# Matmul, scale and add: one tile's results sent in eleven small transfers, and one move done whole

## The chip, the cores and the metric

The kernel runs on one core of one Trainium2 chip. The metric is the device time of one execution in microseconds; the kernel before has a median of 209.18 us over three runs (209.13 to 209.81).

## The reference

`x` is 16 × 512 × 1024, `weight` 1024 × 768, `add_value` 16 × 512 × 768, all float32; `scale` is 0.1.

```python
def reference(x, weight, scale, add_value):
    return (scale * np.matmul(x, weight) + add_value).astype(np.float32)
```

Flattened, it is one product of 8192 × 1024 by 1024 × 768, scaled, with a matrix of the same shape as the result added.

## The kernel before, in words

The 8192 rows are 64 tiles of 128 rows. They lie in three blocks of 24, 24 and 16 tiles. Within a block a partition holds consecutive rows of the matrix, so that a transfer of n neighbouring tiles is 128 contiguous runs of n × 4096 bytes (`x`) or n × 3072 bytes (`add_value` and the results).

**The stream.** All large transfers are written out in `STREAM` (lines 22 to 25): `x0+4` loads tiles 0 to 3 of x, `a` stands for `add_value`, `w` for the weight, `o` for results. SyncE issues them in that order on its one queue (`sync_engine`, line 120). Ahead of an issue it waits, where needed, for the transfer eight places earlier (`lanes`), for the moves that free a slot of x, for the results that free a slot of `ao`, or, ahead of an `o`, for the results to be made (`made`). `x` has 16 tile slots (`xs`). `add_value` and the results share 32 tile slots (`ao`): the result overwrites what was added. The last entry, `o60+4`, is issued on line 243, behind the end of the critical section in which all engines run their own instruction lists, and so behind the last instruction of each engine.

**The moves.** ScalarE and GpSimd (`mover`, line 140) cast x to bf16 and rearrange it into one of two buffers `va`, four tiles (one move q, 0 to 15) at a time; each of the two engines does half of the blocks. A move is eight instructions of 32 partitions and four tiles. Moves listed in `HALVED` (line 17: 0, 1 and 10) are done in two halves of two tiles, sixteen instructions, so that the first two tiles are ready sooner.

**Turn and finish.** VectorE (line 160) transposes two tiles of `va` into `xt` (`turn`), and later makes two tiles of results (`finish`): product × scale + `add_value`, written in place into `ao`, which counts up `made`.

**The product.** TensorE (line 219) runs a loop over the tiles: for each tile 8 steps over k, with two matmuls a step (512 and 256 columns), and releases two tiles at a time through `done`.

A transfer's completion adds 16 to its semaphore. The functions that the change touches:

Of the kernel before, what the change touches and what calls it, by code (L numbers as in the profile page):

```python
# [7 lines left out]
P = 128  # L8
# [5 lines left out]
MM_BUFS = 4  # L14
XT_TILES = 4
LANES = 8
HALVED = (0, 1, 10)
TURN_FIRST = (0, 24)
VA_BUFS = 2
MOVE = 4  # L20

STREAM = """
    x0+4 w0+8 x4+8 a0+8 a8+8 x12+4 x16+8 a16+8 x24+8 a24+8 x32+8 o0+8 o8+8 a32+8 x40+8
    a40+8 x48+8 x56+4 o16+8 o24+8 a48+4 x60+4 a52+4 a56+8 o32+16 o48+4 o52+8 o60+4
"""


# [7 lines left out]
def kernel(  # L35
# [22 lines left out]
    def blocks(flat):  # L58
        return [(s, g, flat[P * s:P * (s + g), :].rearrange("(p t) n -> p t n", t=g))
                for s, g in BLOCKS]  # L60

    x_v, add_v, out_v = blocks(x_f), blocks(add_f), blocks(out_f)
    w_v = weight.rearrange("(p r) n -> p r n", p=P)

    def rows(view, s, n):
        for first, g, block in view:
            if first <= s and s + n <= first + g:
                return block[:, s - first:s - first + n, :]
        raise ValueError((s, n))
# [5 lines left out]
    ao = const.tile([P, A_SLOTS, N], fp32, name="ao")  # L75
    w_bf = const.tile([P, KJ, N], bf16, name="w_bf")
    RUN = K // 4
    va = [const.tile([P, MOVE, 4, RUN], bf16, name=f"va{i}") for i in range(VA_BUFS)]
    xt = const.tile([P, XT_TILES, KC, P], fp32, name="xt")
# [5 lines left out]
    by_act, by_pool, pool_go, turned, casts, done, made = (  # L85
        tc.alloc_semaphore(name)
        for name in ("by_act", "by_pool", "pool_go", "turned", "casts", "done", "made"))
    TURNED = MOVE * VA_BUFS
    MADE = TURNED + MM_BUFS

    def carriers(op, s, n):
        return [mark for (o, a, k), mark in zip(stream, landed)
                if o == op and a < s + n and s < a + k]

    def slots(op, s, n):
        ring = X_SLOTS if op == "x" else A_SLOTS
        k = s % ring
        assert k + n <= ring
        return slice(k, k + n)

    def engine(eng):
        known = {}

        def need(sem, value):
            if known.get(id(sem), 0) < value:
                eng.wait_ge(sem, value)  # L106
                known[id(sem)] = value

        return need

    def transfer(eng, op, s, n):
        if op == "w":
            return eng.dma_start(ao[:, W_SLOT + s:W_SLOT + s + n, :], w_v[:, s:s + n, :])  # L113
        if op == "x":
            return eng.dma_start(xs[:, slots(op, s, n), :], rows(x_v, s, n))  # L115
        if op == "a":
            return eng.dma_start(ao[:, slots(op, s, n), :], rows(add_v, s, n))  # L117
        return eng.dma_start(rows(out_v, s, n), ao[:, slots(op, s, n), :])

    def sync_engine(eng):  # L120
        need = engine(eng)
        for (op, s, n), (sem, mark) in zip(stream, landed):
# [13 lines left out]
            if op == "o":  # L136
                need(made, MADE + last)
            transfer(eng, op, s, n).then_inc(sem, 16)

    def mover(eng, copy, parity, count, go=None):  # L140
        need = engine(eng)
        if go is None:
            eng.preload_act_table(mybir.ActivationFunctionType.Copy)  # L143
        for q in range(MOVES):
            for mark in carriers("x", MOVE * q, MOVE):
                need(*mark)
            if q >= VA_BUFS:
                need(turned, TURNED + MOVE * (q - VA_BUFS + 1))
            if go is not None:
                eng.sem_inc(go, 1)  # L150
            k = MOVE * q % X_SLOTS
            src = xs[:, k:k + MOVE, :].rearrange("p i (b k) -> p i b k", b=4)
            step = MOVE // 2 if q in HALVED else MOVE
            for t in range(0, MOVE, step):
                for a in (parity, parity + 2):
                    for b in range(4):
                        copy(va[q % VA_BUFS][32 * b:32 * b + 32, t:t + step, a, :],  # L157
                             src[32 * a:32 * a + 32, t:t + step, b, :]).then_inc(count, step // 2)

    def vector_engine(eng):  # L160
        need = engine(eng)

        def cast_w(s, n):
            for mark in carriers("w", s, n):
                need(*mark)
            for h in range(s, s + n, 4):
                eng.tensor_copy(w_bf[:, h:h + 4, :], ao[:, W_SLOT + h:W_SLOT + h + 4, :]).then_inc(casts, 4)  # L167

        def turn(pair):
            move, half = divmod(pair, 2)  # L170
            moved = 16 * move + (8 * (half + 1) if move in HALVED else 16)
            need(by_act, moved)
            need(by_pool, moved)
            if pair > 1:
                need(done, 4 * (pair - 1))
            pairs = va[move % VA_BUFS][:, 2 * half:2 * half + 2, :, :].bitcast(fp32)
            eng.transpose(  # L177
                xt[:, 2 * half:2 * half + 2, :, :].rearrange("p i c (a m) -> p i c a m", a=4),
                pairs.rearrange("p i a (k c) -> p i c a k", c=KC),
            ).then_inc(turned, 2)  # L180

        def finish(pair):
            for mark in carriers("a", 2 * pair, 2):
                need(*mark)
            need(done, 4 * (pair + 1))
            a = ao[:, slots("a", 2 * pair, 2), :]
            q = 2 * (pair % 2)
            eng.scalar_tensor_tensor(  # L188
                a, mm[:, q:q + 2, 0:N], float(scale), a,
                op0=mybir.AluOpType.mult, op1=mybir.AluOpType.add).then_inc(made, 2)  # L190

        turn(0)
        for op, s, n in stream:
            if op == "w":
                cast_w(s, n)
        turn(1)
        for pair in range(T // 2):
            ahead = pair + 2 < T // 2
            if ahead and pair in TURN_FIRST:
                need(done, 4 * (pair + 1))  # L200
                turn(pair + 2)
            finish(pair)
            if ahead and pair not in TURN_FIRST:
                turn(pair + 2)
# [14 lines left out]
    def tensor_engine(eng):  # L219
        eng.sem_inc(turned, TURNED)  # L220
        eng.sem_inc(made, MADE)
        eng.wait_ge(casts, KJ)
# [14 lines left out]
    with tc.tile_critical(no_gpsimd_drain=True):  # L237
        sync_engine(nc.sync)
        mover(nc.scalar, nc.scalar.copy, 0, by_act)
        mover(nc.gpsimd, nc.gpsimd.tensor_copy, 1, by_pool, pool_go)  # L240
        vector_engine(nc.vector)
        tensor_engine(nc.tensor)
# [36 lines left out]
```

## Time and profile before

| | |
|---|---|
| median of three runs | 209.18 us |
| profiled execution, its own time | 209.87 us |
| its span | 208.1 us |
| mean granted TensorE clock | 0.981 |
| busy: TensorE, VectorE, ScalarE, GpSimd | 81%, 59%, 67%, 67% |
| data moved | 87.06 MB, 418 GB/s over the span |

Times in the profile count from the start of the span. A row of the timeline gives the start, the duration, the engine, the line and the operation, and in brackets how long the engine was idle before and what released it; "SPq" is the queue work of SyncE, whose instructions here are the issues of transfers. A row of stretches gives the stretch, its length, then busy time and number of instructions for TensorE, its weight loads, VectorE, ScalarE and GpSimd, then the granted clock, the mean busy share of the 16 transfer engines (DMA engines), and GB/s. In the DMA view the digits are the busy share of these engines in 40 equal slices, "packets" are the single pieces that they process, and packets under 512 B are completion signals of 4 bytes. q1 is the queue that SyncE issues on, and q14 carries the fetching of instructions. A group row gives the busy time and the mean duration in ns after the bar, and then idle time with its releasers.

### The profile page before, as it was taken

The page shows a single profiled execution, that of the slowest core. Times are in us where ns is not written, and L with a number is a line of the kernel's source. Part 1 is how long each engine was busy: PE and PEld are TensorE (multiplying, and loading weights), DVE is VectorE, ACT ScalarE, POOL GpSimd, SP SyncE. Part 2 cuts the span into 40 slices and gives each one's busy share as a digit, 9 for nine tenths or more (in the row PEclk, how much of TensorE's full clock was granted, in tenths as well). Part 3 has the DMA queues.
Part 4 walks back from the last instruction along what each step waited for, and adds up shares of the span by engine and source line. Part 5 has one row for each costly group of instructions (what it writes and reads, how often), then busy time and mean ns, then how long its engine had stood idle before and what let it go on. Part 6 is the DMA issues. An engine that isn't in the chain of part 4 may idle for free.

```text
span 208.1 us, 2174 instructions
## 1 busy us (share of the span) xinstructions
PE 167.7 (81%) x1008; PEld 50.4 (24%) x512; DVE 122.9 (59%) x66; ACT 139.3 (67%) x153; POOL 139.9 (67%) x156
## 2 busy tenths in 40 slices
PE   0001994969999999999999999994999999999500
PEld 0000231313333333333333333321333333333100
DVE  0037309646777777777777777738677759776300
ACT  2495199989799896969694069999998969000000
POOL 0399399999799997969694059999999979000000
PEclk9999999999999999999999999999999999999975
DMA  6999999999999999999999999999999999998993
GB/s 249 452 408 447 409 453 444 409 457 403 436 461 409 425 463 416 367 411 439 439 427 438 419 441 450 403 428 447 435 409 432 427 439 449 449 453 364 454 411 161
DMA packets 4035, 87.06 MB, mean 418 GB/s; under 512 B 448, under 2 KB 448, under 8 KB 448
## 3 DMA queue, kind: packets, MB, share of 16 engines
q1 hardware_dynamic: 4032, 87.03, 97.9%
q14 instruction: 3, 0.02, 0.0%
HBM read 61.87 MB, written 25.17 MB: 418 GB/s over the span
## 4 chain that ended last, share of the span: by engine, by line
DMA 43%; PE 25%; POOL 21%; issue 3%; DVE 2%; SPq 1%; POOLq 0%; DVEq 0%
DMA xs<-in_x_dram 31%; POOL va L157 21%; PE mm L232 16%; DMA out_dram<-ao 12%; PE mm L207 9%; DVE xt L177 1%; DVE ao L188 1%; SPq L115 0%; SPq L113 0%; SPq L117 0%; POOLq L150 0%; SPq L106 0%; DVEq L106 0%; SPq L274 0%; SPq L237 0%
## 5 line engine op out<-in xcount | busy, mean ns | idle before, releaser
L232 PE MATMUL mm<-w_bf,xt 128*128 128x512 bf16 x496 | 163.8, 382 | 26.9 <-DVE w_bf L167 19.8
L157 POOL CAST va<-xs 32x1024 bf16<-32x1024 f32 (+1 forms) x152 | 139.7, 919 | 36.8 <-DMA xs<-in_x_dram 22.4
L157 ACT CAST va<-xs 32x1024 bf16<-32x1024 f32 (+1 forms) x152 | 138.0, 908 | 36.6 <-DMA xs<-in_x_dram 23.4
L207 PE MATMUL mm<-w_bf,xt 128*128 128x256 bf16 x512 | 140.2, 274 | 0.8
L232 PEld LDWEIGHTS mm<-w_bf,xt 128*128 128x128 bf16 x512 | 50.4, 98 | 144.6 <-issue 138.7
L177 DVE STREAM_TRANSPOSE xt<-va 128x1024 f32<-128x1024 f32 x32 | 65.2, 2038 | 32.0 <-POOL va L157 30.6
L188 DVE SCALAR_TENSOR_TENSOR ao<-mm,ao 128x1536 f32<-128x1536 f32 x32 | 56.0, 1754 | 42.5 <-PE mm L207 39.4
L167 DVE CAST w_bf<-ao 128x3072 bf16<-128x3072 f32 x2 | 3.8, 1948 | 0.0
L143 ACT ACT_TABLE_LOAD x1 | 1.3, 1283 | 0.9 <-SPq L237 0.9
L260 POOL MEMSET const-float32-0.0<- 128x1 f32 x1 | 0.1, 98 | 0.2 <-issue 0.2
L260 POOL MEMSET const-bfloat16-1.0<- 128x1 bf16 x1 | 0.1, 101 | 0.0
L260 POOL MEMSET const-float32-1.0<- 128x1 f32 x1 | 0.1, 98 | 0.0
L260 POOL MEMSET const-uint8-127<- 128x1 uint8 x1 | 0.1, 98 | 0.0
## 6 DMA issues: line engine op xcount, KB each, us to landing
xs<-in_x_dram SPq DMA_DIRECT2D x6, 4096.0 KB, 20.8
ao<-in_add_value_dram SPq DMA_DIRECT2D x7, 3072.0 KB, 25.2
out_dram<-ao SPq DMA_DIRECT2D x5, 3072.0 KB, 24.8
xs<-in_x_dram SPq DMA_DIRECT2D x4, 2048.0 KB, 13.3
out_dram<-ao SPq DMA_DIRECT2D x1, 6144.0 KB, 33.9
ao<-in_weight_dram SPq DMA_DIRECT2D x1, 3072.0 KB, 14.1
ao<-in_add_value_dram SPq DMA_DIRECT2D x2, 1536.0 KB, 14.6
out_dram<-ao SPq DMA_DIRECT2D x2, 1536.0 KB, 19.8
```

What stands on the lines that cost most here:

```text
L143: eng.preload_act_table(mybir.ActivationFunctionType.Copy)
L157: copy(va[q % VA_BUFS][32 * b:32 * b + 32, t:t + step, a, :], src[32 * a:32 * a + 32, t:t + step, b, :]).then_inc(count, step // 2)
L167: eng.tensor_copy(w_bf[:, h:h + 4, :], ao[:, W_SLOT + h:W_SLOT + h + 4, :]).then_inc(casts, 4)
L177: eng.transpose(xt[:, 2 * half:2 * half + 2, :, :].rearrange("p i c (a m) -> p i c a m", a=4), pairs.rearrange("p i a (k c) -> p i c a k", ...
L188: eng.scalar_tensor_tensor(a, mm[:, q:q + 2, 0:N], float(scale), a, op0=mybir.AluOpType.mult, op1=mybir.AluOpType.add).then_inc(made, 2)
L207: return eng.add_instruction(mybir.InstMatmult(name=nc.get_next_instruction_name(), engine=eng.engine, ins=[eng.lower_ap(weights), eng.low ...
L232: eng.matmul(mm[:, q, 0:CUT], piece, w_bf[:, j, 0:CUT], **flags)
L260: nc = _bacc.Bacc("TRN2", target_bir_lowering=False, num_devices=1)
```

## The change

Tile 47 is taken out of the transfer of results `o32+16`, which becomes `o32+15`. Its 128 rows (one per partition, 3,072 bytes each) are sent by eleven transfers of their own, issued by ScalarE (nine: partitions 5 to 39, four at a time, the last with three) and by GpSimd (two: partitions 0 to 4, and 40 to 127), each behind its last move. Both engines wait for `made` to cover tile 47 first, and for their transfers to land afterwards. They are dealt with the aim that one of the 16 transfer engines gets a single row of tile 47. In the same edit move 10 (tiles 40 to 43) is no longer done in halves.

```diff
-HALVED = (0, 1, 10)
+HALVED = (0, 1)
 TURN_FIRST = (0, 24)
+SPREAD = 47
+BY_ACT = [(a, min(a + 4, 40)) for a in range(5, 40, 4)]
+BY_POOL = [(0, 5), (40, P)]
...
-    a40+8 x48+8 x56+4 o16+8 o24+8 a48+4 x60+4 a52+4 a56+8 o32+16 o48+4 o52+8 o60+4
+    a40+8 x48+8 x56+4 o16+8 o24+8 a48+4 x60+4 a52+4 a56+8 o32+15 o48+4 o52+8 o60+4
...
+    spread_act, spread_few, spread_many = (
+        tc.alloc_semaphore(name) for name in ("spread_act", "spread_few", "spread_many"))
+
+    def spread(eng, a, b):
+        return eng.dma_start(rows(out_v, SPREAD, 1)[a:b], ao[a:b, slots("o", SPREAD, 1), :])
...
+        need(made, MADE + SPREAD + 1)
+        if go is None:
+            for a, b in BY_ACT:
+                spread(eng, a, b).then_inc(spread_act, 16)
+            need(spread_act, 16 * len(BY_ACT))
+        else:
+            for (a, b), sem in zip(BY_POOL, (spread_few, spread_many)):
+                spread(eng, a, b).then_inc(sem, 16)
+            need(spread_few, 16)
+            need(spread_many, 16)
```

The added lines of the last part stand at the end of `mover`, behind its loop; `go` is None for ScalarE.

## The prediction

> **What bounds the kernel now.** I read the page's slices and DMA queues first, then the timeline of each engine from 160 us on, and last the DMA view of short windows at the end of the span.
>
> ```profile
> span 208.1 us, 2174 instructions
> ...
> DMA  6999999999999999999999999999999999998993
> GB/s 249 452 408 447 409 453 444 409 457 403 436 461 409 425 463 416 367 411 439 439 427 438 419 441 450 403 428 447 435 409 432 427 439 449 449 453 364 454 411 161
> DMA packets 4035, 87.06 MB, mean 418 GB/s; under 512 B 448, under 2 KB 448, under 8 KB 448
> ...
> q1 hardware_dynamic: 4032, 87.03, 97.9%
> q14 instruction: 3, 0.02, 0.0%
> ```
>
> The sixteen transfer engines are busy from the first slice to the last: 97.9% of 16 engines' span is packets of the one queue. So the kernel ends when its bytes are through, as long as the last results reach the queue before it runs dry. These rows say that they do:
>
> ```profile
> 154.02 1.76 DVE L188 SCALAR_TENSOR_TENSOR ao<-mm,ao 128x1536 f32<-128x1536 f32 x1 [1.49 <-PE mm L207]
> 168.25 8.52 ACT L157 CAST va<-xs 32x1024 bf16<-32x1024 f32 x8 [1.88 <-DVE xt L177]
> 168.29 8.69 POOL L157 CAST va<-xs 32x1024 bf16<-32x1024 f32 x8 [0.90 <-DVE xt L177]
> 195.62 1.76 DVE L188 SCALAR_TENSOR_TENSOR ao<-mm,ao 128x1536 f32<-128x1536 f32 x1 [3.44 <-PE mm L207]
> 197.66 0.33 SPq L118 DMA_DIRECT2D out_dram<-ao  x1
> ```
>
> VectorE makes the last two tiles by 195.62 + 1.76 = 197.38; the last transfer (tiles 60 to 63) is issued at 197.66. Now the end of the span, in three windows of the DMA view (from 205.3, from 206.1 and from 206.3 us, each to the end; forty slices each, the GB/s of a slice counting the packets that start in it), and stretches ahead of them:
>
> ```profile
> 203.00:204.00 1.00, 0.00 (x0) 0.00 (x0) 0.00 (x0) 0.00 (x0) 0.00 (x0) 0.50 0.98 418
> 204.40:204.80 0.40, 0.00 (x0) 0.00 (x0) 0.00 (x0) 0.00 (x0) 0.00 (x0) 0.50 0.58 246
> 204.80:205.20 0.40, 0.00 (x0) 0.00 (x0) 0.00 (x0) 0.00 (x0) 0.00 (x0) 0.50 0.22 92
> ```
> ```profile
> DMA  4008004004000000400000000000000000000000
> GB/s 176 0 0 351 0 0 176 0 0 176 0 0 0 0 0 0 176 0 0 0 0 0 0 0 0 0 0 0 0 0 0 0 0 0 0 0 0 0 0 0
> DMA packets 9, 0.07 MB, mean 26 GB/s; under 512 B 3, under 2 KB 3, under 8 KB 3
> ...
> DMA packets 3, 0.01 MB, mean 6 GB/s; under 512 B 2, under 2 KB 2, under 8 KB 2
> ...
> DMA packets 2, 0.01 MB, mean 7 GB/s; under 512 B 1, under 2 KB 1, under 8 KB 1
> ```
>
> Until 204.4 all engines move data; after 204.8 about a fifth do. From 205.3 on nine packets start: six of 12,288 bytes (a partition's row of the last transfer, four tiles of 3,072) and three that only signal completion. Three engines are thus late. A slice of the first window is 0.07 us, so the six begin near 205.3, 205.5 (two), 205.7, 205.9 and 206.4. The spacing 205.5, 205.9, 206.4 is one engine's, 0.46 us a packet; it ends at 206.4 + 0.46 = about 206.9 us. The packet at 205.7 ends the second engine at about 206.2 (one signal starts between 206.1 and 206.3), the other one at 205.5 the third at about 206.0. The other thirteen are done before 205.3, most near 204.8. The kernel waits 0.7 us for one engine alone, and some 2 us for three. Its span ends 208.1 − 206.9 = 1.2 us behind the last packet.
>
> The profiled execution took 209.87 us, 1.8 more than its span; the median of the runs is 209.18, 0.69 below. I take the difference that the sum gives from the median.
>
> **Part 1, tile 47 in small transfers.** A row of one tile is 3,072 bytes: at 12,288 bytes in 0.46 us, 0.115 us of an engine. Removed: o32+16 becomes o32+15, each of whose 128 rows is 0.115 us shorter. With 128/16 = 8 rows on each engine that is 8 × 0.115 = −0.92 us everywhere. Added: the same 128 rows, one of them to one engine. That engine's balance is −0.92 + 0.115 = −0.8 us; the other fifteen carry 127 rows, 8.5 each, hence 0 for an engine with eight and +0.23 for one with ten.
>
> By the Trainium skill, page "DMA: Bandwidth & Descriptors", section "Why a DMA increments its semaphore by 16 and not by 1", a transfer runs on the largest number of engines up to 16 that divides its outer size: 4, 3, 5 and 11 here, the lowest-numbered ones for ScalarE's transfers and consecutive ones for GpSimd's. By that rule, if GpSimd's begin at engine 0, engines 0 to 2 get ten rows, engine 3 nine, engine 4 one and engines 5 to 15 eight; no run here shows it yet.
>
> Which engine of the sixteen is the late one no view names. If it is the one with a single row, it ends at 206.9 − 0.8 = 206.1, and the second then sets the end: 206.2 plus what eight separate rows cost above one piece of the same bytes. That price has no row. From below it is 0: a packet of 12 KB moves at the pace of the larger ones (418 GB/s at a share of 0.98 in the stretch 203 to 204; the page's mean is 418 GB/s at 97.9%). From above, the nearest row of a packet that comes in from another queue is an instruction fetch of 8 KB (first fence below: window 58.8 to 59.2; then windows 53.88 to 54.2, 61.3 to 62.2 and 61.65 to 62.2):
>
> ```profile
> q14 instruction: 2, 0.02, 11.8%
> ...
> DMA packets 2, 0.02 MB, mean 77 GB/s; under 512 B 1, under 2 KB 1, under 8 KB 1
> ...
> DMA packets 15, 0.43 MB, mean 473 GB/s; under 512 B 2, under 2 KB 2, under 8 KB 2
> ...
> DMA packets 13, 0.39 MB, mean 715 GB/s; under 512 B 1, under 2 KB 1, under 8 KB 1
> ```
>
> Two fetches take 11.8% of 16 × 0.4 us, 0.76 us, or 0.38 each; 8 KB at the pace above is 0.31, so 0.07 us too many per packet at the least. At 53.88 one completion signal is left; after the fetches two come past 61.3 and one of these past 61.65, which is where the late engine's lag begins. The lag is about half a microsecond more than before, at most 0.2 us per fetch beyond its bytes. So a row's surcharge lies between 0 and 0.2 us. I take 0.01, near the lower end, because rows are packets of the same direction and kind as their neighbours while a fetch is not: 8 × 0.01 = +0.1 us. The second engine then ends at 206.3, and the gain is 206.9 − 206.3 = 0.6 us.
>
> **What the new instructions wait for.** Both movers come to the new lines behind their last move, at 168.25 + 8.52 = 176.8 (ScalarE) and 177.0 (GpSimd); tile 47 is in the results made at 154.02 (pair 23), 20 us before. ScalarE then issues nine transfers; with SP's 0.33 us each (row above) that is 3.0 us, to about 180, on an engine with no other work left. GpSimd issues two. Their price on GpSimd is not in the trace; between 0.3 and a few microseconds it ends by 185. Nothing stands behind these instructions but the end of the critical section, at which SP sends the last transfer. The two waits therefore cost nothing if the rows land before 197.4. The SP queue holds o32+15 (rows of 46 KB, 15 × 0.115 = 1.7 us each, eight per engine), then o48+4 and o52+8. If an engine takes one packet from each queue in turn, nine rows pass while nine or ten large packets do: until about 177 + 9 × 1.7 = 192. The cover is 5 us, and 2 more, since the last transfer's eight packets (3.7 us) begin at 204.5 − 3.7 = 200.8 on the fastest engines, though issued at 197.66. If the cover were gone, each microsecond past about 199 would lengthen the run by one.
>
> **Part 2, tiles 40 to 43 moved whole.**
>
> ```profile
> L157 POOL CAST va<-xs 32x1024 bf16<-32x1024 f32 x104 | 107.6, 1034 | 12.9 <-DVE xt L177 5.7 <-DMA xs<-in_x_dram 1.2
> L157 POOL CAST va<-xs 32x512 bf16<-32x512 f32 x48 | 32.2, 670 | 24.0 <-DMA xs<-in_x_dram 21.3
> ...
> 127.17 2.05 DVE L177 STREAM_TRANSPOSE xt<-va 128x1024 f32<-128x1024 f32 x1 [0.25 <-POOL va L157]
> 141.26 2.01 DVE L177 STREAM_TRANSPOSE xt<-va 128x1024 f32<-128x1024 f32 x1 [3.91 <-POOL va L157]
> ...
> 140.00:143.30 3.30, 0.66 (x5) 0.10 (x1) 2.04 (x2) 3.23 (x4) 3.12 (x4) 1.00 1.00 425
> ...
> 170.57 1.76 DVE L188 SCALAR_TENSOR_TENSOR ao<-mm,ao 128x1536 f32<-128x1536 f32 x1 [2.43 <-DMA ao<-in_add_value_dram]
> ```
>
> The first half of tile 40's move ends at 127.1, so the move began 8 × 0.67 = 5.4 us earlier, near 121.75, and lasts 10.7 in halves; whole it lasts 8 × 1.03 and gaps, 8.7 us: to 130.5. Tiles 40 and 41 are transposed 3.3 us later (130.5 in place of 127.17), so TensorE stalls some 2.7 us near 130. Tiles 44 to 47 are moved 2 us earlier, and the stall of 2.6 us between 140 and 143.3 closes. Sum: within 0.3 us of nothing at 143. And near 170 VectorE waits 2.43 us for a transfer, which resets TensorE's lead whatever it was. The loads that wait for this move (x56) come 2 us earlier into a queue that is full. Cost 0; without the cover of the full queue it would be those 0.3 us.
>
> **Sum.** −0.6 + 0 + 0: 209.18 − 0.6 = 208.6 us.
>
> **The rivals.**
>
> *Rows cost more than their bytes (slower).* Place: the second late engine, or one with ten rows. With a surcharge s an engine of eight rows ends at 206.2 + 8 s; it decides from s = 0.7/8 = 0.09 us, above which the run gets longer than before. At s = 0.2 it ends at 207.8, +0.9: 210.1 us. For it speaks the fetch's 0.07 to 0.2; against it, the 12 KB packets at full pace.
>
> *The rows wait for whole transfers (slower).* If an engine empties what SP queued of one transfer before it takes another queue's packet, ScalarE's rows pass only behind o32+15 (189), o48+4 (193) and o52+8 (201), land at 201 to 202, and the last transfer follows at 202 + 1 + 3.7 = 207 on engines that ended at 204.8, late ones about 208: +1.1, or 210.3 us. The same page of the Trainium skill, section "Queues, rings and completion order", has an engine drain a packet of some 9 to 17 descriptors from one ring before it switches, which would bring this about; the trace speaks against it, for the two fetches (58.8 to 59.2) went through in the middle of a 3 MB load, within 0.4 us of each other.
>
> *The late engine is another one (no change).* The row that is saved is saved where nobody waits. An engine of eight rows leaves the end as it was, +0.1; one of ten gives +0.3: 209.2 to 209.5 us. The lag begins at an instruction fetch, so it should be the same engine in each run, but nothing shows that it is the chosen one.
>
> *The lag is larger in other runs.* Then −0.8 or more counts: 208.3 us and below. The runs are at 209.13, 209.18 and 209.81, so the lag may as well be smaller.
>
> **How the numbers follow.** From run to run this kernel can be told from no change at about 0.3%, 0.63 us, so the likeliest case lies at the edge. Relief as summed: 0.45 (its own range 208.2 to 209.0), 0.31 of it past the edge, 0.14 within. Larger lag: 0.11, all faster. Other engine: 0.15, 0.12 of it within and 0.03 slower. Dear rows: 0.19, 0.15 slower and 0.04 within. Whole transfers: 0.10, slower. So faster 0.42, same 0.30, slower 0.28. The range is 207.9 to 210.1: it leaves out a lag much over a microsecond and the worst of the two slower cases.
>
> **What would show it.** Right: the last stretch of the DMA view has a shorter tail, the last packet near 206.3, with one or two late engines in place of three; the last transfer is still issued at 197.4 to 198. The small transfers show issue-to-landing times under 16 us. TensorE stalls near 130 and not at 140. Wrong: SP's last issue later than 199 (rows behind whole transfers); a broad tail, many engines busy past 205.5 (dear rows); the same single late engine (wrong engine). A fourth instruction fetch late in the run would add about half a microsecond to one engine.

## The result and the profile after

The changed kernel takes 210.42 us (median of 22 runs, 209.48 to 211.39) against 209.58 us for the kernel before (22 runs, 209.07 to 210.27): a ratio of 1.0039, with a 95% interval from 1.0025 to 1.0053. It is 0.8 us slower where 0.6 us faster was forecast.

The profiled execution of the changed kernel happens to be its quickest run (209.48 us), so its span is not to be held against the one before; what differs is how the time is shared out. The page, its span, its packets and its queues (the two new queues are ScalarE's, q10, and GpSimd's, q0):

```profile
span 207.7 us, 2187 instructions
...
DMA packets 4201, 87.06 MB, mean 419 GB/s; under 512 B 530, under 2 KB 530, under 8 KB 614
...
q1 hardware_dynamic: 4032, 86.64, 97.6%
q0 software_dynamic: 96, 0.29, 0.3%
q10 hardware_dynamic: 70, 0.11, 0.1%
q14 instruction: 3, 0.02, 0.0%
```

The same bytes move. The end of the span, from 205.3 us, in the DMA view of the same run:

```profile
DMA  4049000404040000000000000000000000000000
GB/s 205 0 205 410 0 0 0 205 0 205 0 205 0 0 0 0 0 0 0 0 0 0 0 0 0 0 0 0 0 0 0 0 0 0 0 0 0 0 0 0
DMA packets 12, 0.09 MB, mean 36 GB/s; under 512 B 5, under 2 KB 5, under 8 KB 5
```

Twelve packets start after 205.3 where there were nine, and five of them are completion signals where there were three: five engines are late instead of three. The last packet starts near 206.0 and ends near 206.4. So the late engines have become more, not fewer. The timeline's rows of the end (of GpSimd, VectorE and SyncE):

```profile
175.93 1.15 POOL L98 DMA_DIRECT2D out_dram<-ao  x2
194.59 1.76 DVE L207 SCALAR_TENSOR_TENSOR ao<-mm,ao 128x1536 f32<-128x1536 f32 x1 [3.44 <-PE mm L226]
196.64 0.33 SPq L127 DMA_DIRECT2D out_dram<-ao  x1
```

VectorE is done at 196.35 and the last transfer is issued 0.29 us later, as before (0.28): the small transfers do not hold it up here.

**How the rows were really dealt.** One stretch of 1.92 us (184.05 to 185.97) is about one round, in which every engine moves one row of o32+15 (1.70 us) and what comes between from other queues:

```profile
DMA packets 36, 0.84 MB, mean 437 GB/s; under 512 B 2, under 2 KB 2, under 8 KB 20
## 3 DMA queue, kind: packets, MB, share of 16 engines
q1 hardware_dynamic: 16, 0.74, 88.8%
q0 software_dynamic: 16, 0.09, 11.5%
q10 hardware_dynamic: 4, 0.01, 1.2%
```

q1 has 16 packets, one per engine. q0 has 16 too, with 0.09 MB: fifteen packets of 6,144 bytes, that is two rows each, and one of 8 bytes on an engine that gets no row of this transfer. If GpSimd's 88 rows were on eleven engines, a round would have eleven. In all there are 44 packets of two rows: three on each of fourteen engines, and two on one more. The end of one packet is the start of the next on the same engine, so the engines can be told apart by chaining the packets of the trace; the table below is worked out in this way (where two engines' packets start within a few nanoseconds, names can be exchanged). It shows the lag, that is, how much later than the median engine each one came to the end of its share of a transfer, in us: behind a52+4 (near 168.5 us, ahead of all of tile 47's rows, the first of which starts at 174.3), behind o32+15 and at the end; and the bytes that each had from GpSimd:

```
engine   behind   behind    at the   from GpSimd       ScalarE's
         a52+4    o32+15    end                        rows
a         0.62     1.35     1.72     21.5 KB (7 rows)   yes
b         0.56     1.41     1.65     21.5 KB (7 rows)   yes
c         0.30     1.15     1.52     21.5 KB (7 rows)   yes
d         0.51     1.15     1.29     21.5 KB (7 rows)   no
e        -0.49     0.33     0.71     21.5 KB (7 rows)   yes
nine    -0.49 to  -0.50 to -0.49 to  18.4 KB (6 rows)   no
others    0.11     0.11     0.11
one       0.24     0.00     0.00     12.3 KB (4 rows)   no
one       0.08    -0.59    -0.59     no row             no
```

GpSimd's transfer of five rows put one row on each of five engines. Its transfer of 88 rows put six on each of fourteen engines, the first five among them, four on one more, and none on the last. With ScalarE's nine or eight rows, four engines carry 15 or 16 rows of tile 47 in place of 8; the fifth, which was to have one, carries seven; and the engine that was relieved is one that nobody waited for. The four with 15 or 16 rows lose 1.1 to 1.2 us against the median, which has six. Engine d loses 0.8, of which its one row more explains about 0.1; it is the engine whose packets of results take longer (last section). Before the first row came, a, b and d had been the latest of all, and c the next, hardly later than the latest of the others (0.24).

That is what the Trainium skill, page "DMA: Bandwidth & Descriptors", section "Why a DMA increments its semaphore by 16 and not by 1", states as an exception to the rule that the prediction took from it: some plain copies issued by GpSimd run on sixteen engines with the rows divided by 16 and rounded up (88/16 is 5.5, so six). The trace agrees with the exception, with 15 packets a round and 6, 4 and 0 rows, and not with the rule.

### The profile page after: what moved, and what is told of

The parts are those of the page before. It is cut to its first block, busy times and chain, and to the rows that moved or that the text cites. A ratio compares the mean times of both kernels' runs of the same rounds, so it can differ in the third digit from the quotient of the medians.

```text
span 207.7 us, 2187 instructions
## 1 busy us (share of the span) xinstructions
PE 169.1 (81%) x1024; PEld 50.4 (24%) x512; DVE 122.9 (59%) x66; ACT 137.8 (66%) x145; POOL 139.6 (67%) x150
## 4 chain that ended last, share of the span: by engine, by line
PE 50%; DMA 23%; POOL 13%; DVE 5%; ACT 2%; issue 1%; SPq 0%; DVEq 0%; POOLq 0%; ACTq 0%
PE mm L251 33%; DMA xs<-in_x_dram 23%; PE mm L226 17%; POOL va L166 13%; DVE xt L196 3%; ACT va L166 2%; DVE ao L207 2%; SPq L122 0%; SPq L124 0%; DVEq L115 0%; POOLq L159 0%; ACTq L115 0%; SPq L293 0%; SPq L256 0%; SPq L115 0%
## 5 line engine op out<-in xcount | busy, mean ns | idle before, releaser
L251 PE MATMUL mm<-w_bf,xt 128*128 128x512 bf16 x512 | 168.7, 382 | 25.4 <-DVE w_bf L186 19.9
L166 POOL CAST va<-xs 32x1024 bf16<-32x1024 f32 (+1 forms) x144 | 138.3, 960 | 37.3 <-DMA xs<-in_x_dram 21.5
L166 ACT CAST va<-xs 32x1024 bf16<-32x1024 f32 (+1 forms) x144 | 136.5, 948 | 37.1 <-DMA xs<-in_x_dram 22.6
L98 POOL DMA_DIRECT2D out_dram<-ao x2 | 1.2, 584 | 0.0
```

What stands on the lines that cost most here:

```text
L98: return eng.dma_start(rows(out_v, SPREAD, 1)[a:b], ao[a:b, slots("o", SPREAD, 1), :])
L251: eng.matmul(mm[:, q, 0:CUT], piece, w_bf[:, j, 0:CUT], **flags)
```

## The experiments

All times are medians beside runs of the kernel before on the same chip; "+0.1 us" is the difference from it, or, where the text says so, the difference by the ratio, which is worked out from all runs and can differ from that of the medians. The theories are named in the expectations: A, that the dealing of the rows costs; B, the whole move; C, packets from a second queue as such; D, GpSimd's transfers as such; then A', that the late engines are among those that transfers of few rows run on; E, that which engines are late is chance; later F, A with the load that the table shows; G, that the rows land late and hold up the last transfer.

**Only the whole move.**

```diff
-HALVED = (0, 1, 10)
+HALVED = (0, 1)
```

> Only the move of tiles 40 to 43 is done whole; tile 47 leaves with the others in o32+16 as before. Theory A (the loss is the dealing of tile 47's rows: the engines that get nine or ten rows are late ones, and each row costs more than its bytes): no change, within 0.2 us of the kernel before. Rival B (the whole move costs it): 0.5 to 0.9 us longer, as the change. Either way TensorE's stall should stand near 130 us and not at 140.

Measured: 209.34 against 209.33 us, ratio 0.9998 (0.9989 to 1.0007). B falls.

**Only the eleven transfers.** The changed kernel with `HALVED = (0, 1, 10)`.

> Only tile 47's eleven transfers; move 10 stays in halves. Theory A: all of the loss, 0.5 to 0.9 us above the kernel before. Rival B: no change.

Measured: 210.57 against 209.33 us, ratio 1.0052 (1.0038 to 1.0066). The loss is here. By the ratio it is 1.1 us (0.8 to 1.4), above the 0.5 to 0.9 that were expected and above that of the whole change (0.8; 0.5 to 1.1), though the intervals overlap; why it is larger is open. In its profiled run one of the engines with ScalarE's rows was already 2.1 us late before tile 47's rows, and 3.2 at the end. VectorE is done at 199.79 there and the last transfer is issued at 200.07, so that the rows do not hold it up.

**One transfer of 128 rows from ScalarE.**

```diff
-BY_ACT = [(a, min(a + 4, 40)) for a in range(5, 40, 4)]
-BY_POOL = [(0, 5), (40, P)]
+BY_ACT = [(0, P)]
```

with the lines for GpSimd left out.

> The change, but tile 47 leaves in one transfer of 128 rows from ScalarE, eight rows to every engine, none from GpSimd. Theory A with uneven dealing as the cause: within 0.3 us of the kernel before. Rival C (any packets from a second queue cost some 0.08 us each, whoever gets them): eight rows on every engine, 0.5 to 0.7 us longer. Rival D (GpSimd's transfers cost it): no change.

Measured: 209.40 against 209.33 us, ratio 1.0004 (0.9995 to 1.0013). A transfer from a second queue costs nothing that can be measured here (0.3 us at most by the interval), if it is even.

**Eight transfers of 16 rows from ScalarE.** As the one above, with `BY_ACT = [(a, a + 16) for a in range(0, P, 16)]`.

> The change, but tile 47 leaves in eight transfers of 16 rows from ScalarE, one row of each to every engine. The dealing is even, the rows are as single as in the change. Theory A with single rows dear (0.08 us each above their bytes): 0.5 to 0.8 us longer than before on every engine. If it is the uneven dealing alone that costs: within 0.3 us of before.

Measured: 209.44 against 209.33 us, ratio 1.0006 (0.9998 to 1.0015). Single rows with a signal each are not dear. C falls, and with it the surcharge of the prediction's first rival: over eight rows it is 0.1 us (0.3 at most by the interval), near the 0.01 us a row that the sum took. The packets say the same: in the first profile of the change each of ScalarE's rows takes 0.121 us and its signal 0.009, where the prediction had 0.115 for the row.

**Which engines are late.** Fourteen tiny loads (2 to 15 rows, into a buffer of their own) at the end of the kernel mark the engines: the more of them run on an engine, the more of the loads' engines it belongs to.

```diff
     transfer(nc.sync, *stream[-1])
+    for n in range(2, 16):
+        nc.sync.dma_start(mark[0:n, n, :], x_f[0:n, 0:16])
```

> The kernel before, and behind its last transfer fourteen tiny loads from SyncE (2, 3, ... 15 rows of 64 bytes, into a buffer of their own), so that the engine on which a packet runs can be told by how many of them follow on it. Its time is a few microseconds longer for that and not compared. Theory A' (the instruction fetches run on low-numbered transfer engines, so that the change gave most rows to late ones): the engines that lose time at the fetches near 58 and 108 us are among those with 12 to 14 of the tiny loads. Rival E (which engines are late is random, or spread over all sixteen): they carry any number, 0 to 14.

> The same once more. Theory A': the same engines are late. Rival E: others.

> The changed kernel with the same fourteen tiny loads at its end. Theory A': the late engines of its end (0.9 us or more behind the median) are the four with most of ScalarE's rows, and they were late before tile 47's rows came; the engine with one row was an ordinary one.

Measured: 213.78 and 213.38 us, and 213.80 for the changed kernel, the loads included. There are 119 packets of 64 bytes, 2 + 3 + ... + 15, and as many more completion signals than without the loads, so that a load of n rows runs on n engines. In the second of these runs, chained as above:

```
lag behind the median engine, us     what came on it        loads right behind
behind o52+8 (run m2)
1.23                                 a fetch at 59.6 us      7 of 7
1.07                                 0.2 to 0.4 us lost in   7 of 7
                                     each transfer of results
                                     up to o32+16
0.64                                 a fetch at 109.3 us     7 of 7
0.37                                 a fetch at 60.2 us      7 of 7
0.11 to -0.53 (the other twelve)     nothing                 fewer, where it could be told
```

The seven loads that follow at once have 5 to 11 rows; an engine with all seven serves even the one of five rows. So the four late engines are all among those that serve the smallest transfers. Three are late since an instruction fetch, one loses time in writes. In the first run, as in the kernel with the whole move alone, the same four kinds are the late ones, at 1.18, 1.18, 0.79 and 0.69 us behind o52+8 in the first. For the late engines of these runs chance (E) falls. In the marked run of the changed kernel five engines are late at o48+4, at 2.00, 1.91, 1.42, 1.21 and 0.79 us; its loads could be assigned to the engines only in part, and the engine without a row of GpSimd had been an ordinary one (0.09).

**GpSimd's transfers as they are, ScalarE's nearly even.**

```diff
-BY_ACT = [(a, min(a + 4, 40)) for a in range(5, 40, 4)]
+BY_ACT = [(5, 37), (37, 40)]
```

> The change with GpSimd's two transfers as they are, but ScalarE's 35 rows in one transfer of 32 (two rows on every engine) and one of three. Theory F (the trace of the change shows GpSimd's 88 rows as six per engine on the first engines and none on the last, not eight on eleven engines; so engines 0 to 3 carried 15 or 16 rows, and three of them are the late ones): engines 0 to 2 now carry ten rows and the rest eight or nine, so 0 to 0.3 us above the kernel before. Rival D (GpSimd's transfers themselves cost it): 0.7 to 1.2 us above, as the change.

Measured: 209.55 against 209.22 us, ratio 1.0012 (1.0001 to 1.0022), that is +0.25 us by the ratio. Most of the loss goes, although GpSimd does what it did in the change. D falls.

**The uneven load without GpSimd.** `BY_ACT` is that of the change and `[(40, 120), (120, P), (0, 5)]` behind it, all from ScalarE.

> The change without GpSimd: ScalarE sends its nine small transfers, and the other 93 rows in transfers of 80, 8 and 5 rows. Engines 0 to 2 carry 16 rows, engine 3 fifteen, engine 4 seven, 5 to 7 six, 8 to 15 five. Theory F: the same loss as the change, 0.7 to 1.2 us above the kernel before. Rival D: no change.

Measured: 210.47 against 209.22 us, ratio 1.0054 (1.0036 to 1.0071). The time is as F forecast, but the profile shows another way to it. Two rows of the timeline (of VectorE and SyncE) and stretches of its last microseconds:

```profile
195.46 1.76 DVE L200 SCALAR_TENSOR_TENSOR ao<-mm,ao 128x1536 f32<-128x1536 f32 x1 [3.44 <-PE mm L219]
...
202.78 0.33 SPq L125 DMA_DIRECT2D out_dram<-ao  x1
...
198.00:200.00 2.00, 0.00 (x0) 0.00 (x0) 0.00 (x0) 0.00 (x0) 0.00 (x0) 0.85 1.07 461
200.00:202.00 2.00, 0.00 (x0) 0.00 (x0) 0.00 (x0) 0.00 (x0) 0.00 (x0) 0.50 0.33 140
202.00:203.00 1.00, 0.00 (x0) 0.00 (x0) 0.00 (x0) 0.00 (x0) 0.00 (x0) 0.50 0.12 49
204.00:205.00 1.00, 0.00 (x0) 0.00 (x0) 0.00 (x0) 0.00 (x0) 0.00 (x0) 0.50 0.96 406
```

VectorE is done at 197.22 and the last transfer leaves only at 202.78; in between the engines run dry, a share of 0.33 and then 0.12. The last of ScalarE's signals lands at 202.1. Here the rows do hold up the last transfer: with twelve transfers in one queue, and each row and each signal taking a turn of its own against a large packet (chained, they alternate one for one), the cover is gone. At the end the sixteen engines finish within 0.3 us of each other, so it is not a few late ones that set the end. This run is thus no evidence for F. It prices the prediction's second slow rival in another form, and raised the question (G) whether the change loses in the same way.

**Half the unevenness.** ScalarE alone, `BY_ACT = [(a, a + 4) for a in range(0, 16, 4)] + [(16, P)]`: eleven rows on four engines and seven on the others.

> Half the unevenness, from ScalarE alone: four transfers of four rows and one of 112. Engines 0 to 3 carry eleven rows, all others seven. Theory F, by 0.115 us a row for three rows more on the late engines: 0.3 to 0.5 us above the kernel before. If unevenness cost in another way (a threshold, or the number of transfers): either nothing or the whole 0.7 to 1.2 us.

Measured: 209.82 against 209.22 us, ratio 1.0020 (1.0007 to 1.0033), +0.4 us by the ratio (0.15 to 0.7), 0.6 between the medians, where F forecast 0.3 to 0.5. In its profile VectorE is done at 196.54 and the last transfer is issued at 196.82, not held up. Chained, the four engines with eleven rows fall 0.49 us further behind than the eleven ordinary ones with seven, between a52+4 and the end: 0.12 us for each of four rows with its signal. The loss grows with the rows on these engines.

**The same rows, earlier.** Both engines issue them ahead of their last move; the waits stay at the end.

```diff
         for q in range(MOVES):
+            if q == MOVES - 1:
+                need(made, MADE + SPREAD + 1)
+                ... (the eleven transfers)
```

> The change, but both engines issue tile 47's rows ahead of their last move (near 165 us in place of 171 to 177), so that they land well before the last transfer is issued; the waits for them stay at the end. Theory F (the load on engines 0 to 3): the same loss as the change, 0.7 to 1.2 us above the kernel before, since the same engines carry the same rows. Rival G (the rows land so late that the last transfer waits for them): back to the kernel before, within 0.2 us. Loads of add_value in the queue at that time could be held up by the rows, which would add a little to the loss.

Measured: 210.01 against 209.31 us, ratio 1.0035 (1.0021 to 1.0049). VectorE's last instruction and the last issue:

```profile
195.75 1.76 DVE L210 SCALAR_TENSOR_TENSOR ao<-mm,ao 128x1536 f32<-128x1536 f32 x1 [3.44 <-PE mm L229]
...
197.80 0.33 SPq L127 DMA_DIRECT2D out_dram<-ao  x1
```

The last of ScalarE's signals lands at 175.2, more than 20 us ahead of the end, nothing is held up, and the loss of 0.7 us is still that of the change. G falls; F stands.

**The changed kernel again.**

> The changed kernel once more, for a second look at its end. Theory F: the last packets are those of the engines with nine of ScalarE's rows, and the last transfer is issued about 0.3 us after VectorE's last instruction, hence not held up by the rows. Rival G: the last transfer is issued a microsecond or more after VectorE is done.

Measured: 210.10 us in its one run, span 208.3. The same two rows, and the end from 205.3 us:

```profile
196.79 1.76 DVE L207 SCALAR_TENSOR_TENSOR ao<-mm,ao 128x1536 f32<-128x1536 f32 x1 [3.44 <-PE mm L226]
...
198.83 0.33 SPq L127 DMA_DIRECT2D out_dram<-ao  x1
```
```profile
DMA  3070330330300300300000000000000000000000
GB/s 154 0 307 0 154 154 0 154 154 0 154 0 0 154 0 0 154 0 0 0 0 0 0 0 0 0 0 0 0 0 0 0 0 0 0 0 0 0 0 0
DMA packets 15, 0.12 MB, mean 38 GB/s; under 512 B 5, under 2 KB 5, under 8 KB 5
```

Issued 0.28 us after VectorE's end (198.55), while ScalarE's last signal lands at 195.7. Five signals and ten rows start after 205.3, the last near 206.6: five late engines again. Chained, they are again the four with ScalarE's rows, 2.43, 2.22, 1.81 and 1.12 us behind the median engine at the end, and one with seven rows and none of ScalarE's, 1.61 behind.

## Why the prediction was wrong

- **What bounds the kernel** was right: the transfer engines set the end, by the latest of them. Both profiles of the changed kernel, the one before and those of the experiments read that way, but for the twelve transfers.
- **The step that failed is the deal, "the other fifteen carry 127 rows, 8.5 each, hence 0 for an engine with eight and +0.23 for one with ten".** The rows lay 15 or 16 on four engines, 7 on the fifth, 6 on nine, 4 and 0 on the last two. Seven or eight rows more than the eight of before are 0.8 to 0.9 us at the prediction's own 0.115 us; against the median engine, which now has six, nine or ten more rows are 1.0 to 1.15, and 1.1 to 1.2 was measured. The price per row was right and the number of rows wrong.
- **"If it is the one with a single row"**: it was not. The engine that was to have one row carried seven, and the relieved one had been ordinary. Worse, of the four that got ScalarE's rows a and b were late already, and c a little, for both come from the same end: transfers of few rows run on the same few engines on which the instruction fetches had left their lag. The prediction saw the fetches and did not ask which engines they share with a transfer of four rows. Its third rival, the wrong engine, was the right mechanism but priced with at most ten rows: 209.2 to 209.5 us, against a measured loss of 0.8.
- **A row's surcharge** of 0.01 us was right (eight transfers of 16 rows: 0.1 us in all; 0.121 us for a row's packet and 0.009 for its signal), and the fetch was a poor model for it. The fetch itself was also read too low. The prediction compared the latest engine before the fetches with the latest one after them, and so found half a microsecond in all. By the packets one fetch sets its engine back by 0.7 to 0.9 us, some 0.4 to 0.6 beyond its bytes and not 0.2 at most. The sum did not use that bound.
- **The waits** cost nothing, as forecast, but the cover was thinner: rows and signals take a turn each, so that ScalarE's last signal lands at 194.1 in the first profile, not 192. ScalarE issued from 170.5 on, beside its last move, not behind it at 176.8.
- **The rows behind whole transfers** fell: in the round shown, three rows and a signal of ScalarE's and fifteen packets of GpSimd's pass beside one packet of o32+15 on each engine.
- **The whole move** was right: no change by itself. Rows of the changed kernel show where the stall went:

```profile
129.84 2.01 DVE L196 STREAM_TRANSPOSE xt<-va 128x1024 f32<-128x1024 f32 x1 [2.83 <-POOL va L166]
139.10 2.07 DVE L196 STREAM_TRANSPOSE xt<-va 128x1024 f32<-128x1024 f32 x1
...
169.69 1.76 DVE L207 SCALAR_TENSOR_TENSOR ao<-mm,ao 128x1536 f32<-128x1536 f32 x1 [2.56 <-DMA ao<-in_add_value_dram]
...
128.00:133.00 5.00, 3.44 (x22) 0.98 (x10) 3.16 (x2) 4.88 (x6) 4.75 (x5) 1.00 0.97 419
138.00:143.00 5.00, 5.00 (x33) 1.56 (x16) 3.58 (x3) 4.90 (x5) 4.70 (x6) 1.00 1.04 442
```

TensorE loses 1.6 us near 130 (2.7 was forecast) and none between 138 and 143, and near 170 VectorE waits 2.56 us for a transfer, as before (2.43).

No run here deals the rows as the change meant to, and none beats the kernel before. Whether sparing the late engines would pay is therefore not tested: the transfers tried either load all engines alike or add to the ones that were late. Nor is the opposite, a load of the same unevenness on engines that were not late; that it would cost less follows from the price per row, but no run shows it.

## What to carry to other kernels

When a kernel waits for its transfer engines, ask of every small transfer how many engines it runs on and which; few rows mean few engines, here the same ones as were late already, and the loss was each extra row's bytes on them. Count the packets of one round in the trace before relying on a deal, since the rows of a GpSimd transfer and of a ScalarE one are not divided in the same way. And count a transfer's signal as a turn in its queue: many small transfers behind large ones land late, which costs nothing until the last large one must wait for them.

## What was not expected of the hardware

- GpSimd's copy of 88 rows went out as 44 packets of two rows, three on each of fourteen engines, two on the next and none on the last; the one of five rows as one row on each of five engines.
- The late engines are late for lasting reasons. An instruction fetch of 8 KB (three within the span) sets an engine back by 0.7 to 0.9 us: it takes 0.31 to 0.45 us itself, and a packet beside it 0.35 to 0.55 longer than its like. One engine loses 0.2 to 0.4 us in each transfer of results up to o32, and about 0.1 or less in each of the last three. Nothing in the rest of the run made it up. Why that engine is slower in writes stays open.
- Tile 47 in eight transfers of 16 single rows, each row with a signal of its own, cost 0.1 us in all, so the packets' number was not the price; where they lay was.
